# GpSimd sums pairs 0, 3, 4 and 5 of the attention probabilities, and the queries' second products of layer 0 come one pair of output tiles later

## The chip, the cores and the metric

The kernel runs on one core of a Trainium2 chip. A core has five engines that run their own instruction streams in order and wait for each other by semaphores: TensorE (PE in the profile, with its weight loads PEld), VectorE (DVE), ScalarE (ACT), GpSimd (POOL) and SyncE (SP), which here issues most of the transfers. The metric is the device time of one execution in microseconds. Before the change the median of three runs is 2087.75 us (2087.69 to 2091.03).

## The reference

One step of a two-layer trunk over 2048 latent tokens and 128 context tokens, width 1024, all in float32. Cut to what the change touches, layer 0 is:

```python
q_lat, kv_lat, k_pe, gate_a, pool_in, gate_b = jnp.split(h @ w_in, SPLITS_AB, axis=-1)
q = (rmsnorm(q_lat, q_norm) @ w_uq).reshape(B, T, MLA_HEADS, QK_NOPE + QK_ROPE)
ckv = rmsnorm(kv_lat, kv_norm)
...
s = (jnp.einsum('bqhd,bkhd->bhqk', qn, k_nope, preferred_element_type=jnp.float32)
     + jnp.einsum('bqhr,bkr->bhqk', qp, k_pe, preferred_element_type=jnp.float32))
p = jax.nn.softmax(s * sm_scale, axis=-1).astype(v.dtype)
return jnp.einsum('bhqk,bkhd->bqhd', p, v)
```

There are 4 heads, and each latent query sees 2048 latent and 128 context keys. `q_lat` has 256 columns and `w_uq` is the queries' second matrix. The softmax needs, for every query, the sum of its probabilities over 2176 keys. Layer 1 is a gated position-mixing block and is not touched.

## The kernel before

Activations are held with features on the 128 partitions and tokens along the row. Exact float32 products are made of three fast ones: every operand is split into a high part (a ScalarE cast) and a low part (a VectorE or GpSimd subtraction, `sub`, line 160), and `mm3` (lines 175 to 179) issues high x high, high x low and low x high.

Layer 0's projection goes over five blocks of tokens (512, 512, 512, 384, 256). In each, `linear` makes *output pairs*: two output tiles of 128 features in one double PSUM buffer (`psA`, two buffers of two banks), 48 products of 128x512 a pair. The order in a block is: keys' latent pair, queries' latent pair, then six more pairs (pooling input and two gates), which I number 1 to 6. After each of these six a hook runs: it lets every coroutine in `hold` (`kv_consume`, `q_consume`), the next block's preparation (`n`), the pooling (`p`) and the late modulation (`l`) take one step each. `q_consume` (line 529) normalises the queries' latent, splits it into `qh` (line 548) and `ql`, and then gives the queries' second products in three steps of 12 products, with a `yield` between the steps: heads 0 and 1, heads 2 and 3, and the rotary part. Each step takes a `psA` buffer, evacuates it by a ScalarE cast (line 561) and a VectorE subtraction, and SyncE stores the results to `q_d`. The pairs 1 to 6 are evacuated by ScalarE (line 591). Weights come in tiles of 512 KB through four raw buffers, split by line 423 (ScalarE) and line 160 (VectorE).

Attention then goes over 17 blocks: 16 of 512 latent queries of one head, and one for the context queries. A block has nine steps: eight *pairs* of key tiles (0 to 7, two tiles of 128 keys) and one single tile (the context keys of the cache). For a pair, TensorE makes the scores into `psA` (lines 820 to 824), ScalarE copies them to SBUF (line 835), and VectorE keeps a running maximum from PSUM (line 845), so a `psA` buffer is free only after both. When a block's scores are complete, TensorE turns the maximum (line 851), VectorE reduces it (853), TensorE spreads it over the partitions (859), VectorE subtracts it pair by pair (865) and ScalarE takes the exponent (867). All pairs but pair 4 are split for the product with the values: ScalarE casts (871), GpSimd subtracts (873). The products with the values run 14 steps behind the scores.

The sum of the probabilities is shared out: pairs in `POOL_SUM` (for the very first block `POOL_FIRST`) are added on GpSimd (lines 883 and 886) into one SBUF tile, the others on VectorE (889 and 892) into a PSUM bank (`psE`), and at the end VectorE adds GpSimd's part (896). The result is split, summed over the partitions by TensorE (921, 922), inverted on VectorE (295, 302, 303), and GpSimd multiplies it with the gate (928).

A scheduler of the framework sets the order on each engine from the program order and from when it thinks operands are there; each engine then runs its stream strictly in that order.

Of the kernel before, what the change touches and what calls it, by code (L numbers as in the profile page):

```python
# [12 lines left out]
ALU = mybir.AluOpType  # L13
# [68 lines left out]
AHEAD = 3  # L82
PT = 512
FIRST_W = (7, 9)
POOL_SUM = (1, 3, 4, 6)
POOL_FIRST = (1, 4)
SPLIT_PV = (0, 1, 2, 3, 5, 6, 7)
SPLIT_LAST = ()

# [24 lines left out]
def trunk_kernel(ctx, tc, xT, cols_in, cond_in, ident_in, edge_in, rope_in, w_ada, w_ada_T, w_in_t, w_inp_T, w_pool,  # L114
# [20 lines left out]
    def wt(dt=F32, shape=(P, 2, 512)):  # L135
        return wpool.tile(list(shape), dt, tag="w", name=nm("w"))
# [7 lines left out]
    def et(dt=F32, shape=(P, 2, 512)):  # L144
        return epool.tile(list(shape), dt, tag="e", name=nm("e"))
# [4 lines left out]
    def ps_pair(shape=(P, 2, 512)):  # L150
        return psA.tile(list(shape), F32, tag="A", name=nm("psA"))

    def ps1(tag, shape=(P, 512)):
        return psS.tile(list(shape), F32, tag=tag, name=nm("ps" + tag))

    def f(ap):
        return ap.bitcast(F32)

    def sub(eng, out, a, hi):
        eng.tensor_tensor(out=out, in0=a, in1=f(hi), op=ALU.subtract)  # L160

    V, S, G, PE = nc.vector, nc.scalar, nc.gpsimd, nc.tensor
# [3 lines left out]
    def store(c, *a):  # L166
        qs[c].dma_start(*a)

    def behind(ins, last):

        if last is not None:
            tc.add_manual_dep(ins.ins, last.ins.name, NO_SYNC, reason="issue order")
        return ins

    def mm3(ps, w, x, first, last):

        PE.matmul(ps, w[0], x[0], start=first, stop=False)  # L177
        PE.matmul(ps, w[0], x[1], start=False, stop=False)  # L178
        PE.matmul(ps, w[1], x[0], start=False, stop=last)  # L179
# [106 lines left out]
    def split1(x, n, alloc, lo_eng=None):  # L286

        t = alloc(F32R)
        S.copy(t[:, 0, :n], x)
        sub(lo_eng or V, t[:, 1, :n], x, t[:, 0, :n])  # L290
        return t
# [14 lines left out]
    def total(x, n, pool):  # L306

        if not pool:
            return split1(x, n, et)
        r = et()  # L310
        G.partition_all_reduce(r[:, 0, :n], x, P, bass_isa.ReduceOp.add)
        return r

    def rstd(r, n, d, pool, tag):

        if pool:
            return invert(r[:, 0, :n], r, n, 1.0 / d)
        ps = ps1(tag)
        PE.matmul(ps[:, :n], ones[1], r[:, 0, :n], start=True, stop=False)
        PE.matmul(ps[:, :n], ones[1], r[:, 1, :n], start=False, stop=True)  # L320
        return invert(ps[:, :n], et(), n, 1.0 / d)
# [166 lines left out]
    def rope(raw, n, ns, tab):  # L488

        t = et()  # L490
        if ns:
            V.stream_shuffle(t[:, 1, :ns], raw[:, :ns], [i ^ 16 for i in range(32)])
            V.tensor_tensor(out=t[:, 0, :ns], in0=raw[:, :ns], in1=tab[:, 0, :ns], op=ALU.mult)
            (G if ROPE_G else V).tensor_tensor(out=t[:, 1, :ns], in0=t[:, 1, :ns], in1=tab[:, 1, :ns], op=ALU.mult)
            V.tensor_tensor(out=t[:, 0, :ns], in0=t[:, 0, :ns], in1=t[:, 1, :ns], op=ALU.add)
        if ns < n:
            V.tensor_copy(out=t[:, 0, ns:n], in_=raw[:, ns:n])
        return t[:, 0, :n]
# [34 lines left out]
    def q_consume(bi, ps, tab):  # L533
        o, n = BLOCKS[bi]
        ns = min(n, DEC - o)
        q = et()
        S.copy(q[:, :, :n], ps[:, :, :n])
        sq = et()
        S.activation(out=sq[:, :, :n], in_=ps[:, :, :n], func=AF.Square)
        V.tensor_tensor(out=sq[:, 0, :n], in0=sq[:, 0, :n], in1=sq[:, 1, :n], op=ALU.add)  # L540
        hl = total(sq[:, 0, :n], n, AR_Q)
        yield
        r = rstd(hl, n, 256, AR_Q, "D")
        for a in range(2):
            V.scalar_tensor_tensor(out=q[:, a, :n], in0=q[:, a, :n], scalar=cols[:, C_QN + a:C_QN + a + 1],
                                   in1=r, op0=ALU.mult, op1=ALU.mult)
        qh = et(F32R)
        S.copy(qh[:, :, :n], q[:, :, :n])
        ql = et(F32R)
        sub(V, ql[:, :, :n], q[:, :, :n], qh[:, :, :n])  # L550
        yield
        for hp in range(2):
            if hp:
                yield
            pq = ps_pair()
            for a in range(2):
                for k in range(2):
                    mm3(pq[:, a, :n], (g.wc[0][:, k, 2 * hp + a], g.wc[1][:, k, 2 * hp + a]),
                        (qh[:, k, :n], ql[:, k, :n]), k == 0, k == 1)
            th = et(F32R)  # L560
            S.copy(th[:, :, :n], pq[:, :, :n])
            tl = et(F32R)
            sub(V, tl[:, :, :n], pq[:, :, :n], th[:, :, :n])
            for a in range(2):
                store(ST_QH, q_d[2 * hp + a, :, 0, o:o + n], f(th[:, a, :n]))
                store(ST_QL, q_d[2 * hp + a, :, 1, o:o + n], f(tl[:, a, :n]))
        yield
        pq = ps_pair()
        for hp in range(2):
            for k in range(2):  # L570
                mm3(pq[:, hp, :n], (g.wpe[0][:, k, hp], g.wpe[1][:, k, hp]),
                    (qh[:, k, :n], ql[:, k, :n]), k == 0, k == 1)
        raw = et()
        S.copy(raw[:, :, :n], pq[:, :, :n])
        for hp in range(2):
            pe = rope(raw[:, hp, :n], n, ns, tab)
            t = et(F32R)
            S.copy(t[:, 0, :n], pe)
            sub(V, t[:, 1, :n], pe, t[:, 0, :n])
            for a in range(2):  # L580
                for part in range(2):
                    store(ST_QP, q_d[2 * hp + a, 64 * part:64 * part + 64, 2, o:o + n], f(t[64 * a:64 * a + 64, part, :n]))
# [162 lines left out]
    for bi, (o, n) in enumerate(BLOCKS):  # L745
# [26 lines left out]
        linear(hh, n, 1, lambda p, ps: start(kv_consume, ps))  # L772
        hook(HOOK_KV)
        linear(hh, n, 1, lambda p, ps: start(q_consume, ps))
        drain(hold[0], 1)
        hook(HOOK_Q)
# [84 lines left out]
    def step_exp(b, p):  # L861

        nt = len(b.tiles[p])
        s = b.s[p]
        V.tensor_tensor(out=s[:, :nt], in0=s[:, :nt], in1=b.m[:, None, :].broadcast_to([P, nt, QB]),  # L865
                        op=ALU.subtract)
        S.activation(out=s[:, :nt], in_=s[:, :nt], func=AF.Exp, scale=SM_SCALE)  # L867
        b.parts[p] = low = None
        if p in (SPLIT_LAST if b.j == 15 else SPLIT_PV) and nt == 2:
            ph = wt(F32R)  # L870
            S.copy(ph[:, :nt], s[:, :nt])  # L871
            pl = wt(F32R)
            low = behind(G.tensor_tensor(out=pl[:, :nt], in0=s[:, :nt], in1=f(ph[:, :nt]), op=ALU.subtract), g.gated)  # L873
            b.parts[p] = ph, pl
        if p == 0:
            b.pool = b.acc = None
        last_p = len(b.tiles) - 1
        if nt == 1 and p == 0:
            b.total = s[:, 0]
        elif p in (POOL_SUM if b.j else POOL_FIRST):  # L880
            if b.pool is None:
                b.pool = et()
                behind(G.tensor_tensor(out=b.pool[:, 0], in0=s[:, 0], in1=s[:, 1], op=ALU.add), low)
            else:
                for a in range(2):
                    behind(G.tensor_tensor(out=b.pool[:, 0], in0=b.pool[:, 0], in1=s[:, a], op=ALU.add), low or g.gated)  # L886
        elif b.acc is None:
            b.acc = ps1("E")
            V.tensor_tensor(out=b.acc, in0=s[:, 0], in1=s[:, 1], op=ALU.add)
        else:  # L890
            for a in range(nt):
                V.tensor_tensor(out=b.acc, in0=b.acc, in1=s[:, a], op=ALU.add)
        if p == last_p:
            if b.acc is not None:
                b.total = b.acc
                V.tensor_tensor(out=b.total, in0=b.acc, in1=b.pool[:, 0], op=ALU.add)
            b.hl = split1(b.total, QB, et)
            b.gt = et()
            if b.h is not None:
                store(LD_GT, b.gt[:, 0], ga_d[b.h, :, b.t0:b.t0 + QB])  # L900
            else:
                dma(b.gt[:, 0].rearrange("p (h n) -> p h n", h=H), ga_d[:, :, DEC:T].rearrange("h p n -> p h n"))
# [39 lines left out]
    for j in range(16):  # L942
        b = Blk()
# [6 lines left out]
    b = Blk()  # L950
# [317 lines left out]
    for i in range(len(steps) + LAG + PV_BEHIND + 2):  # L1268
        if 0 <= i - LAG < len(steps):
            step_exp(*steps[i - LAG])  # L1270
# [5 lines left out]
        if i < len(steps):  # L1276
            b, p = steps[i]
# [13 lines left out]
        if 0 <= j < len(steps):  # L1291
            b, p = steps[j]
# [134 lines left out]
```

## Time and profile before

| what | value |
|---|---|
| runs | 2087.75 us median (2087.69 to 2091.03) |
| profiled execution: time, span | 2087.39 us, 2085.6 us |
| TensorE busy | 2001.2 us, 96% of the span |
| VectorE, ScalarE, GpSimd busy | 70%, 53%, 28% |
| mean granted TensorE clock | 0.989 |
| layer 0's projection, attention, the rest | about 0 to 515, 515 to 1095, 1095 to 2086 us |

The span runs from the first to the last instruction; 1.8 us of the execution lie around it. "Idle before" in a row is the time for which the engine had nothing to run just before, and the arrow names what ended it.

### The profile page before, as it was taken

What the parts mean: (1) busy time and instruction counts of PE and PEld (TensorE: products, weight loads), DVE (VectorE), ACT (ScalarE), POOL (GpSimd) and SP (SyncE); (2) the same over time, 40 slices, a digit from 0 to 9 for tenths busy, and PEclk for the clock granted to TensorE, in tenths of its full rate; (3) what the DMA queues carried; (4) which work ended last, traced back from release to release, by engine and by line L of the source; (5) the groups of instructions that cost most, each with busy time, mean ns of one, the idle gap of its engine ahead of it and who ended that gap; (6) DMA issues with size and microseconds to landing.
All of it is one profiled execution on the core that took longest, in us unless ns stands there. A gap on an engine that the chain in (4) does not pass through costs nothing.

```text
span 2085.6 us, 26154 instructions
## 1 busy us (share of the span) xinstructions
PE 2001.2 (96%) x9652; PEld 1666.0 (80%) x9652; DVE 1469.1 (70%) x2222; ACT 1098.6 (53%) x1285; POOL 580.7 (28%) x405
## 2 busy tenths in 40 slices
PE   6898999999999999999989999999999999999997
PEld 3787777998777777777758788888888888889997
DVE  4688977665887878878784898455665556477575
ACT  4634444544676767667664545443355335445555
POOL 1003020111478686868771120001101100010000
PEclk9999999999999999999999999999999999999999
DMA  9577767676111011101124564334524542364463
GB/s 355 191 259 244 242 226 233 211 227 191 45 31 47 30 46 31 46 30 33 49 86 162 174 210 147 116 131 162 172 83 141 190 142 101 122 224 160 129 222 126
DMA packets 123696, 300.62 MB, mean 144 GB/s; under 512 B 12144, under 2 KB 39088, under 8 KB 123568
## 3 DMA queue, kind: packets, MB, share of 16 engines
q1 hardware_dynamic: 105168, 258.58, 37.3%
q10 hardware_dynamic: 13728, 23.60, 3.7%
q0 software_dynamic: 4672, 16.78, 2.3%
q8 instruction: 76, 1.25, 0.2%
q14 instruction: 52, 0.43, 0.1%
HBM read 243.23 MB, written 55.67 MB: 143 GB/s over the span
## 4 chain that ended last, share of the span: by engine, by line
PE 66%; DVE 12%; POOL 7%; issue 5%; ACT 4%; DMA 3%; SPq 0%; DVEq 0%; POOLq 0%; ACTq 0%
PE psA L178 18%; PE psA L179 18%; PE psA L177 18%; POOL e L886 4%; DVE h L865 3%; POOL w L873 2%; DVE run L845 2%; DVE w L160 2%; PE psB L915 1%; ACT h L835 1%; PE psA L820 1%; PE psA L821 1%; PE psA L824 1%; PE psA L823 1%; PE psA L822 1%
## 5 line engine op out<-in xcount | busy, mean ns | idle before, releaser
L177 PE MATMUL psA<-h,w 128*128 128x512 f32 (+2 forms) x1600 | 575.7, 360 | 9.1 <-ACT e L591 6.6
L179 PE MATMUL psA<-h,w 128*128 128x512 f32 (+2 forms) x1600 | 573.2, 359 | 0.2 <-DVE w L160 0.2
L160 DVE TENSOR_TENSOR w<-r,w 128x1024 fp32r<-128x1024 f32 x280 | 349.2, 1250 | 291.4 <-PE psA L178 214.0
L178 PE MATMUL psA<-h,w 128*128 128x512 f32 (+2 forms) x1536 | 548.8, 357 | 2.0 <-DVE h L160 2.0
L423 ACT CAST w<-r 128x1024 fp32r<-128x1024 f32 x280 | 292.0, 1049 | 240.5 <-PE psA L179 189.2
L177 PEld LDWEIGHTS psA<-h,w 128*128 128x128 f32 x1600 | 302.9, 189 | 49.8 <-ACT e L591 7.3
L179 PEld LDWEIGHTS psA<-h,w 128*128 128x128 f32 x1600 | 302.8, 189 | 38.3 <-DVE w L160 0.4
L178 PEld LDWEIGHTS psA<-h,w 128*128 128x128 f32 x1536 | 290.9, 189 | 38.4 <-DVE h L160 3.1
L873 POOL TENSOR_TENSOR w<-h,w 128x1024 fp32r<-128x1024 f32 x105 | 252.1, 2402 | 132.4 <-ACT w L871 130.5
L845 DVE TENSOR_TENSOR run<-psA,run 128x512 f32<-128x512 f32 x240 | 163.4, 681 | 15.2 <-ACT h L835 14.5
L867 ACT ACTIVATE h<-h 128x1024 f32<-128x1024 f32 (+1 forms) x145 | 143.7, 1014 | 53.1 <-DVE h L865 52.9
L865 DVE TENSOR_TENSOR h<-h,psC 128x1024 f32<-128x1024 f32 (+1 forms) x145 | 163.5, 1145 | 0.9 <-PE psC L859 0.9
L835 ACT COPY h<-psA 128x1024 f32<-128x1024 f32 (+1 forms) x145 | 138.3, 964 | 34.1 <-PE psA L824 33.8
L178 PE MATMUL psA<-o,w 128*128 128x512 f32 (+2 forms) x368 | 134.0, 366 | 0.0
L886 POOL TENSOR_TENSOR e<-e,h 128x512 f32<-128x512 f32 x92 | 120.2, 1307 | 5.8 <-ACT h L867 2.2
L871 ACT CAST w<-h 128x1024 fp32r<-128x1024 f32 x105 | 110.5, 1054 | 11.0 <-PE psB L179 10.9
L639 POOL TENSOR_TENSOR pl<-pl 128x527 f32<-128x527 f32 (+2 forms) x16 | 22.0, 1374 | 329.4 <-PE psA L179 118.9
L179 PE MATMUL psA<-o,w 128*128 128x512 f32 (+2 forms) x304 | 109.1, 361 | 0.0
L177 PE MATMUL psA<-o,w 128*128 128x512 f32 (+2 forms) x304 | 108.9, 361 | 0.0
L177 PE MATMUL psA<-w,h 128*128 128x512 f32 x272 | 106.7, 393 | 1.2 <-ACT o L1147 1.2
L178 PE MATMUL psA<-w,h 128*128 128x512 f32 x272 | 106.1, 390 | 0.1
L179 PE MATMUL psA<-w,h 128*128 128x512 f32 x272 | 105.8, 390 | 0.0
(297 smaller groups left out, 3559.7 us busy)
## 6 DMA issues: line engine op xcount, KB each, us to landing
r<-in_w_inc_t_dram SPq DMA_DIRECT2D x80, 512.0 KB, 3.5
r<-in_w_in_t_dram SPq DMA_DIRECT2D x60, 512.0 KB, 4.1
r<-in_w_oap_t_dram SPq DMA_DIRECT2D x40, 512.0 KB, 3.4
r<-in_w_incv_t_dram SPq DMA_DIRECT2D x40, 512.0 KB, 4.1
r<-in_w_outc_t_dram SPq DMA_DIRECT2D x40, 512.0 KB, 3.5
r<-in_w_ada_T_dram SPq DMA_DIRECT2D x32, 512.0 KB, 4.5
r<-wp_d SPq DMA_DIRECT2D x20, 512.0 KB, 5.9
h<-in_w_ada_dram SPq DMA_DIRECT2D x16, 512.0 KB, 10.5
```

The lines of the kernel that those rows point to most:

```text
L160: eng.tensor_tensor(out=out, in0=a, in1=f(hi), op=ALU.subtract)
L177: PE.matmul(ps, w[0], x[0], start=first, stop=False)
L178: PE.matmul(ps, w[0], x[1], start=False, stop=False)
L179: PE.matmul(ps, w[1], x[0], start=False, stop=last)
L423: S.copy(hi, raw)
L835: S.copy(s[:, :nt], ps[:, :nt])
L845: V.tensor_tensor(out=b.max, in0=ps[:, a], in1=s[:, 0] if p == 0 else b.max, op=ALU.max)
L865: V.tensor_tensor(out=s[:, :nt], in0=s[:, :nt], in1=b.m[:, None, :].broadcast_to([P, nt, QB]), op=ALU.subtract)
L867: S.activation(out=s[:, :nt], in_=s[:, :nt], func=AF.Exp, scale=SM_SCALE)
L871: S.copy(ph[:, :nt], s[:, :nt])
L873: low = behind(G.tensor_tensor(out=pl[:, :nt], in0=s[:, :nt], in1=f(ph[:, :nt]), op=ALU.subtract), g.gated)
L886: behind(G.tensor_tensor(out=b.pool[:, 0], in0=b.pool[:, 0], in1=s[:, a], op=ALU.add), low or g.gated)
```

## The change

It has three parts. `POOL_SUM` becomes pairs 0, 3, 4, 5 (and `POOL_FIRST` 0 and 4), so GpSimd's tile begins with pair 0, VectorE's bank with pair 1, and GpSimd's last pair is 5 in place of 6. VectorE's first addition of a block, which added two SBUF tiles into `psE`, becomes a ScalarE copy of the first tile into `psE` and a VectorE addition of the second to it. And in `q_consume` one more `yield` stands ahead of the first step of the second products.

```diff
-POOL_SUM = (1, 3, 4, 6)
-POOL_FIRST = (1, 4)
+POOL_SUM = (0, 3, 4, 5)
+POOL_FIRST = (0, 4)
...
         ql = et(F32R)
         sub(V, ql[:, :, :n], q[:, :, :n], qh[:, :, :n])
+        yield
         yield
         for hp in range(2):
             if hp:
...
         elif b.acc is None:
             b.acc = ps1("E")
-            V.tensor_tensor(out=b.acc, in0=s[:, 0], in1=s[:, 1], op=ALU.add)
+            S.copy(b.acc, s[:, 0])
+            V.tensor_tensor(out=b.acc, in0=b.acc, in1=s[:, 1], op=ALU.add)
         else:
             for a in range(nt):
                 V.tensor_tensor(out=b.acc, in0=b.acc, in1=s[:, a], op=ALU.add)
```

Lines after the new `yield` are numbered one higher in the changed kernel, and those after the new copy two higher.

The first place is GpSimd in one attention block in the middle of the stage. `w` is the low part of a pair's probabilities (line 873, in the changed kernel 874), `h` a pair's probabilities, the `e` of lines 883 and 886 (884, 887) is GpSimd's sum, and the `e` of line 928 (930) the gate of the block before. Before:

```order
L873 TENSOR_TENSOR w_6077<-h_5721,w_6075 128x1024
L873 TENSOR_TENSOR w_6106<-h_5753,w_6104 128x1024
L883 TENSOR_TENSOR e_6108<-h_5753 128x512
L873 TENSOR_TENSOR w_6140<-h_5788,w_6138 128x1024
L928 TENSOR_TENSOR e_6045<-e_6045,e_6131 128x512
L873 TENSOR_TENSOR w_6177<-h_5817,w_6175 128x1024
L886 TENSOR_TENSOR e_6108<-e_6108,h_5817 128x512 x2
L886 TENSOR_TENSOR e_6108<-e_6108,h_5846 128x512
L873 TENSOR_TENSOR w_6233<-h_5884,w_6231 128x1024
L886 TENSOR_TENSOR e_6108<-e_6108,h_5846 128x512
L873 TENSOR_TENSOR w_6256<-h_5917,w_6254 128x1024
L886 TENSOR_TENSOR e_6108<-e_6108,h_5917 128x512 x2
```

And in the changed kernel, in the block at the same place:

```order
L874 TENSOR_TENSOR w_6082<-h_5725,w_6080 128x1024
L884 TENSOR_TENSOR e_6084<-h_5725 128x512
L874 TENSOR_TENSOR w_6111<-h_5757,w_6109 128x1024
L874 TENSOR_TENSOR w_6146<-h_5792,w_6144 128x1024
L930 TENSOR_TENSOR e_6050<-e_6050,e_6137 128x512
L874 TENSOR_TENSOR w_6183<-h_5821,w_6181 128x1024
L887 TENSOR_TENSOR e_6084<-e_6084,h_5821 128x512 x2
L887 TENSOR_TENSOR e_6084<-e_6084,h_5851 128x512 x2
L874 TENSOR_TENSOR w_6239<-h_5889,w_6237 128x1024
L887 TENSOR_TENSOR e_6084<-e_6084,h_5889 128x512 x2
L874 TENSOR_TENSOR w_6262<-h_5922,w_6260 128x1024
L874 TENSOR_TENSOR w_6294<-h_5949,w_6292 128x1024
```

GpSimd has the same 15 instructions a block; its sum is complete one line-874 subtraction earlier, ahead of the low part of pair 6.

The second place is ScalarE in a block after its maximum is known. `psA` of line 835 (836) are scores, line 867 (868) the exponents, 871 (872) the casts of pairs, `psE` VectorE's sum. Before:

```order
L867 ACTIVATE h_6546<-h_6546 128x1024
L835 COPY h_6888<-psA_6877 128x1024
L871 CAST w_6900<-h_6546 128x1024
L867 ACTIVATE h_6578<-h_6578 128x1024
L867 ACTIVATE h_6613<-h_6613 128x1024
L835 COPY h_6917<-psA_6906 128x1024
L871 CAST w_6929<-h_6578 128x1024
L867 ACTIVATE h_6642<-h_6642 128x1024
L871 CAST w_6963<-h_6613 128x1024
```

And in the changed kernel:

```order
L868 ACTIVATE h_6277<-h_6277 128x1024
L836 COPY h_6620<-psA_6609 128x1024
L872 CAST w_6632<-h_6277 128x1024
L868 ACTIVATE h_6309<-h_6309 128x1024
L868 ACTIVATE h_6344<-h_6344 128x1024
L836 COPY h_6649<-psA_6638 128x1024
L872 CAST w_6661<-h_6309 128x1024
L890 COPY psE_6665<-h_6309 128x512
L872 CAST w_6696<-h_6344 128x1024
```

The copy into `psE` stands behind the cast of pair 1, eighth from the exponent of pair 0; VectorE's addition that needs it stands in VectorE's stream behind the subtractions (line 866) of pairs 0 to 5.

The third place is TensorE in layer 0's second block. `psA_1561` is pair 2, the products on `wch` and `wcl` are the first step of the queries' second matrix, and the products on `h` and `w` of pair 3 follow. Before:

```order
L179 MATMUL psA_1561<-h_1017,w_1447 128x512
L521 MATMUL psD_1613<-ident,e_1277 128x128 x4
L177 MATMUL psA_1619<-e_1512,wch 128x512
L178 MATMUL psA_1619<-e_1514,wch 128x512
L179 MATMUL psA_1619<-e_1512,wcl 128x512
```

And in the changed kernel:

```order
L179 MATMUL psA_1561<-h_978,w_1447 128x512
L521 MATMUL psD_1613<-ident,e_1277 128x128 x4
L177 MATMUL psA_1664<-h_733,w_1551 128x512
L178 MATMUL psA_1664<-h_736,w_1551 128x512
L179 MATMUL psA_1664<-h_733,w_1553 128x512
```

Pair 3 (`psA_1664`) runs whole, 48 products, and the second products start behind it. On ScalarE its evacuation has moved too. Before, in the same block, from the cast of the first step's result on:

```order
L561 CAST e_1632<-psA_1619 128x1024
L361 ACTIVATE h_1642<-h_1284,mod 128x512 x2
L361 ACTIVATE h_1760<-h_1286,mod 128x512
L423 CAST w_1781<-r_1779 128x1024
L361 ACTIVATE h_1760<-h_1286,mod 128x512
L591 ACT_TABLE_LOAD
L591 ACTIVATE e_1734<-psA_1685 128x1024
```

And in the changed kernel, where line 592 evacuates pair 3:

```order
L423 CAST w_1660<-r_1658 128x1024
L361 ACTIVATE h_1621<-h_1284,mod 128x512 x2
L423 CAST w_1760<-r_1758 128x1024
L361 ACTIVATE h_1739<-h_1286,mod 128x512 x2
L592 ACT_TABLE_LOAD
L592 ACTIVATE e_1713<-psA_1664 128x1024
L562 CAST e_1729<-psA_1716 128x1024
```

The evacuation of pair 3 stands behind the same four activations of the next block's preparation (line 361) as before, while the cast of the first step's result has moved from ahead of them to behind it.

## Rows read from the trace of the kernel before

**Rows 1.** The page, its first line.

```profile
span 2085.6 us, 26154 instructions
```

**Rows 2.** Waits of TensorE, whole span: engine line waited for: us, times, longest.

```profile
PE psA L820 <- DVE run L845: 15.6, 30, 1.2
...
PE psA L177 <- ACT e L548: 7.8, 2, 5.9
...
PE psA L178 <- DVE e L160: 4.5, 3, 2.8
PE psB L178 <- POOL w L873: 3.2, 2, 2.6
```

**Rows 3.** Timeline, TensorE, attention: start, us, instruction, [idle before <- what ended it].

```profile
820.07 1.05 PE L859 MATMUL psC<-ident,s 128*128 128x128 f32 x8
821.53 0.50 PE L820 MATMUL psA<-r,K 128*128 128x512 f32 x1 [0.40 <-DVE run L845]
...
829.67 0.47 PE L820 MATMUL psA<-r,K 128*128 128x512 f32 x1 [0.59 <-DVE run L845]
...
837.88 0.39 PE L820 MATMUL psA<-r,Kb 128*128 128x512 f32 x1
```

**Rows 4.** Timeline, VectorE, the same block.

```profile
818.51 0.70 DVE L896 TENSOR_TENSOR psE<-psE,e 128x512 f32<-128x512 f32 x1 [5.26 <-POOL e L886]
...
823.03 2.34 DVE L865 TENSOR_TENSOR h<-h,psC 128x1024 f32<-128x1024 f32 x2
825.37 0.70 DVE L889 TENSOR_TENSOR psE<-h 128x512 f32<-128x512 f32 x1
...
828.84 0.68 DVE L845 TENSOR_TENSOR run<-psA,run 128x512 f32<-128x512 f32 x1
...
835.32 0.65 DVE L845 TENSOR_TENSOR run<-psA,run 128x512 f32<-128x512 f32 x1
```

**Rows 5.** Timeline, GpSimd, the same block.

```profile
805.83 4.09 POOL L886 TENSOR_TENSOR e<-e,h 128x512 f32<-128x512 f32 x3
809.88 2.41 POOL L873 TENSOR_TENSOR w<-h,w 128x1024 fp32r<-128x1024 f32 x1
...
815.82 2.65 POOL L886 TENSOR_TENSOR e<-e,h 128x512 f32<-128x512 f32 x2
...
837.91 1.30 POOL L928 TENSOR_TENSOR e<-e,e 128x512 f32<-128x512 f32 x1 [0.88 <-DVE e L303]
```

**Rows 6.** Timeline, ScalarE, the same block.

```profile
810.81 0.59 ACT L835 COPY h<-psA 128x512 f32<-128x512 f32 x1
...
829.88 1.05 ACT L871 CAST w<-h 128x1024 fp32r<-128x1024 f32 x1
```

**Rows 7.** Timeline, VectorE, layer 0.

```profile
185.37 1.53 DVE L540 TENSOR_TENSOR e<-e 128x512 f32<-128x512 f32 x1
...
209.48 1.23 DVE L160 TENSOR_TENSOR e<-e,e 128x1024 fp32r<-128x1024 f32 x1
```

**Rows 8.** Timeline, GpSimd, layer 0.

```profile
184.97 1.38 POOL L639 TENSOR_TENSOR pl<-pl 128x519 f32<-128x519 f32 x1 [6.51 <-DVE pl L655]
```

**Rows 9.** Timeline, TensorE, layer 0, blocks 0 and 1.

```profile
104.90 0.50 PE L177 MATMUL psA<-h,w 128*128 128x512 f32 x1 [3.71 <-ACT e L591]
...
209.50 0.80 PE L177 MATMUL psA<-e,wch 128*128 128x512 f32 x1 [5.91 <-ACT e L548]
...
229.04 0.40 PE L177 MATMUL psA<-h,w 128*128 128x512 f32 x1
```

**Rows 10.** Stretch, TensorE: length, busy (count), granted clock, DMA share, GB/s.

```profile
209.50:215.50 6.00, 5.54 (x13) 0.53 0.53 175
```

**Rows 11.** Stretch, VectorE, the same columns.

```profile
210.00:313.00 103.00, 87.79 (x151) 0.97 0.72 237
```

**Rows 12.** Timeline, ScalarE, layer 0, block 1.

```profile
226.55 1.28 ACT L591 ACT_TABLE_LOAD   x1 [3.05 <-PE psA L179]
227.85 1.03 ACT L591 ACTIVATE e<-psA 128x1024 f32<-128x1024 f32 x1
```

## The prediction

> **What bounds the kernel now.** I read the page's first line and busy shares, then TensorE's waits over the span, then a timeline of one attention block on four engines, then the waits of layer 0 on their timelines. The profiled execution took 2087.4 us, 0.4 below the median of the runs: its span of 2085.6 [rows 1] and 1.8 around it. The sum below is made against 2087.4. TensorE is busy for 96% of the span, so time can only come from its gaps, from stretches at a lower granted clock, or be lost by new gaps. Its largest group of gaps is line 820, scores waiting for the running maximum of line 845: 15.6 us in 30 waits [rows 2]. Two stand in a block, 0.40 at 821.53 and 0.59 at 829.67 [rows 3], and 30 are two in each of 15 blocks. In layer 0 the first products with the queries' second matrix wait 7.8 us for their high parts and 4.5 for their low parts [rows 2], the largest 5.91 at 209.50, and at 104.90 a pair waits 3.71 for an evacuation [rows 9]: together 16.0.
>
> Where do the waits on line 845 come from? VectorE stood for 5.26 us until 818.51 in front of line 896, which adds GpSimd's sum [rows 4]. GpSimd's last two additions begin at 815.82 and take 2.65 [rows 5], so they end at 818.47. From there VectorE has work without a gap up to the maximum at 828.84, whose end at 829.52 releases TensorE's scores of 829.67 [rows 3, 4]. VectorE waits early in the block, and TensorE pays late in it, because VectorE starts the block's burst with a backlog.
>
> **Pairs 0, 3, 4, 5.** GpSimd keeps its count of instructions. What changes is that no addition waits for pair 6: all are done ahead of that pair's low part, which takes 2.41 [rows 5]. So line 896 can follow about 2.4 us earlier, at 816.1 instead of 818.5 on the old clock. GpSimd also begins with pair 0's sum of 1.3 us (half of 2.65 [rows 5]) in time in which it idles now between the low parts of pairs 0 and 1. The burst behind line 896 then is no longer what TensorE waits for: 2.4 us of advance stand against waits of 0.40 and 0.59. What is late next? The subtractions of line 865 need line 859 of TensorE, which begins at 820.07 and takes 1.05 [rows 3]; they can begin at 821.1, and not at 823.03 [rows 4], because the maxima ahead of them were part of the backlog. That is 1.9 us, still more than 0.59. GpSimd's product with the gate, which waits 0.88 for VectorE's line 303 [rows 5], moves forward with it. I count all of 15.6, and give the term bounds of 12 and 17.6: below, if TensorE keeps a quarter of them; above, if small waits beside them go too.
>
> A second gap follows at the end of the stage: TensorE waits up to 2.6 us for GpSimd's last low part (3.2 in two waits [rows 2]). It comes earlier by the idle time that the first sum now fills, 1.3 us, and by the earlier line 303, up to 0.88 [rows 5]. I take 2.0, bounds 0 and 2.6.
>
> **The copy into psE.** VectorE's addition at 825.37, 0.70 long, stays as one addition; ScalarE gets one 128x512 copy more. No row shows such a copy into PSUM. The nearest is 0.59 for one out of PSUM [rows 6]; bounds 0 (hidden) and all that a late copy would hold. ScalarE is busy for about half of the time, so its own 0.59 costs nothing. What the copy can hold is VectorE: it stands behind the cast of pair 1, which begins at 829.88 and takes 1.05 [rows 6], so the copy would end at 831.5 on the old clock. With the subtractions 1.9 us earlier it ends near 829.6. VectorE reaches its addition behind six subtractions of 1.17 (2.34 for two) and four maxima of 0.6, near 821.1 + 7.0 + 2.4 = 830.5. So the copy is there, with 0.9 to spare. And if it isn't: behind the addition stand the maxima of pair 4, of which the last now ends at 835.97 (835.32 and 0.65 [rows 4]), 1.9 ahead of the scores of pair 6 at 837.88 [rows 3]. With 2.5 of advance, less about 1.0 (0.40 and 0.59) by which TensorE comes earlier, the slack there is 3.4. I take 0.
>
> A row bears on why the addition may want a PSUM operand. In layer 0 a VectorE addition of two SBUF tiles (line 540) took 1.53 us at 185.37 [rows 7], while GpSimd ran line 639 from 184.97 for 1.38 [rows 8]; it ended 0.55 after that one. Line 889, of the same kind and size, takes 0.70 at 825.37 [rows 4], where GpSimd is idle. The Trainium skill ("SBUF — State Buffer", section "SBUF: two separate sides") says that a VectorE instruction with two SBUF inputs and a GpSimd instruction that reads SBUF exclude each other for a whole instruction; the trace agrees. By that rule the old two-SBUF addition, moved to pair 1, would meet a low part of 2.4 us, inside the slack of 3.4: the sum would be the same with and without the copy.
>
> **The extra yield.** In the changed order pair 3 runs ahead of the second products, so their normalised input has a pair's time more. Pair 3 ran for about 11 us, from 215.5 to the end at 226.55 for which its evacuation waits [rows 10, 12]. That covers the 5.91 and the 0.46 behind it (209.50 is followed by another short wait, a part of the 4.5). While TensorE restarts, it also runs slow: from 209.5 to 215.5 the granted clock is 0.53, about the lower of its two levels, which costs 6.0 x (1 - 0.53) = 2.8 us [rows 10]. If all gaps go, and up to 2.8 behind each of the three large ones, that is 16.0 + 8.4 = 24.4: the ceiling.
>
> I don't take the ceiling, since another wait takes the place. Pair 4 needs the second psA buffer again, so pair 3's evacuation, and that stands on ScalarE behind four activations of line 361, which VectorE's line 357 feeds. VectorE ends `ql` at 209.48 + 1.23 = 210.7 [rows 7]. Behind it come 13 instructions up to the fourth line 357: two weight splits of about 1.15, ten of about 0.65, one of 0.15, together 8.9. Then one activation (0.7), the table load (1.28) and the evacuation (1.03) [rows 12]: 210.7 + 11.9 = 222.6. Before, pair 4 began at 229.04 [rows 9], and it had two steps of second products ahead of it, of which one (2.7, 12 of 48 products' 11 us) now runs behind pair 4: 226.3 to compare. That leaves 3.7, of which a new restart at the low clock takes 2.8: 0.9. What is added is how much earlier VectorE itself comes: it is busy for 87.8 of 103 us [rows 11], so of the 3.71 and the slow stretch behind it in block 0 (up to 2.8) it can follow with perhaps half, 3. In block 2 the same order stands with a smaller gap (2.8 is the longest on line 160 [rows 2]): 1. The last gap of 1.3 in block 3 goes. Sum 0.9 + 3 + 1 + 1.3, rounded to 6; bounds -3 (a longer wait for pair 3's evacuation, with its slow restart) and 24.4. I take the value near the lower end, since line 357's chain is a row of work that nothing shortens. The stores to `q_d` on SP come one pair later as well; attention begins long after them, so they cost nothing.
>
> **Sum.** 2087.4 - 15.6 - 2.0 - 6.0 + 0 = 2063.8, say 2064.
>
> **The rivals.**
> (a) Layer 0 gives its ceiling. For it: the gaps of 16.0 are plain, and VectorE has 15 us of idle time in a block. Against it: the walk above. 2087.4 - 17.6 - 24.4 = 2045.
> (b) Half the waits on line 845 stay, because VectorE's queue itself is full there (gapless for 11 us now), and layer 0 gives nothing. 2087.4 - 7.8 - 2.0 = 2078. For it: the changed order puts five subtractions nearly in a row. Against it: 1.9 us of advance against 0.59.
> (c) Slower: the copy into psE comes late. Its place is ScalarE's queue behind the cast of pair 1; should that cast have to wait for a low-part buffer that TensorE's products free, the copy slips by a step. A step is some 3.9 us (TensorE's 829.67 to 837.88 are two [rows 3], 4.1 each). VectorE at 830.5 would be held to about 829.6 + 2 x 4.1 = 837.8 by a slip of two, 7.3 late, which is 3.9 over the slack, of which I take a half in each of 16 blocks since later gaps of VectorE give some back: 31, with nothing gained on line 845: 2087.4 + 31 - 8 = 2110. It decides from 3.4 us of lateness on; by one slip (0.3 over the slack) the cost would be 5 and the time still below before.
> (d) It doesn't do what it says: line 896 waits as long, now for VectorE's own additions of pairs 6 and 7, which it gathers at the end of a block. The additions are as many as before (8 a block), so this would only move the wait; 2087.
>
> **Chances.** The forecast 0.58, with a range of its own from 2055 to 2077 (terms 12 to 17.6, 0 to 2.6, -3 to 12, of which not all fall to one side); (a) 0.15, (b) 0.15, (c) 0.06, (d) 0.06. The range 2049 to 2080 takes in the forecast, (b) and half of the way to (a). About 0.2%, 4.2 us, is what a measurement of this kernel can tell from no change. Faster by more: the forecast, (a) and (b), 0.88; within: (d), 0.06; slower: (c), 0.06.
>
> **What would show it.** In the changed profile: VectorE's idle time in front of line 898 shorter than 5.26 by 2 or more; TensorE's group of line 821 waiting for line 846 gone or under 3 us; GpSimd's last addition ended before pair 6's low part; no idle time on VectorE that ends with a ScalarE copy of line 890. In layer 0: no wait of line 177 on the high part `e`, and in block 1 a new one of the pair behind pair 3 on line 592. Wrong would be the forecast if line 891 waits for the copy in every block, if the waits on line 846 stay above 8 us, or if layer 0 ends later than now.

## The result and the profile after

The changed kernel takes 2057.52 us (median of five runs, 2053.45 to 2060.05) against 2088.28: a ratio of 0.9849, interval 0.9834 to 0.9863, or 31 us less. The forecast was 2064 (24 less), range 2049 to 2080. The profiled execution is the fastest of the five, 2053.45, so its trace shows 34 us less than the trace of before.

The page's first line, TensorE's waits over the span, and one line of its waits before that the rows don't show:

```profile
span 2051.7 us, 26144 instructions
```

```profile
PE psA L177 <- ACT e L592: 16.1, 4, 6.2
...
PE psA L821 <- DVE run L846: 5.8, 6, 1.8
...
PE psB L178 <- POOL w L874: 2.3, 2, 1.6
```

```profile
PE psA L177 <- ACT e L591: 6.6, 3, 3.7
```

Against [rows 2]: the group of line 845 (now 846) fell from 15.6 us in 30 waits to 5.8 in 6, the two groups of the queries' high and low parts (7.8 and 4.5) are gone, and the group on the evacuation of a pair grew from 6.6 us in 3 waits (line 591, the last line shown) to 16.1 in 4 (line 592).

I cut both spans at the same instructions of TensorE. First before, then after: attention from its first to its last spreading of a maximum (line 859, now 860), and the seam from there to the first line 320 of layer 1.

```profile
530.23:1065.24 535.01, 518.32 (x2239) 1.00 0.12 39
1065.24:1177.96 112.72, 107.21 (x421) 0.95 0.49 161
```

```profile
524.39:1036.86 512.47, 510.69 (x2239) 1.00 0.13 40
1036.86:1145.94 109.08, 104.27 (x421) 1.00 0.52 170
```

| stretch | before | after | difference |
|---|---|---|---|
| start, to line 319 in block 0 | 81.28 | 80.97 | -0.3 |
| from there to the same place in block 1 | 109.93 | 104.32 | -5.6 |
| block 1 to block 2 | 108.47 | 107.41 | -1.1 |
| block 2 to block 3 | 97.05 | 98.68 | +1.6 |
| block 3 to the first spreading of a maximum | 133.50 | 133.01 | -0.5 |
| attention | 535.01 | 512.47 | -22.5 |
| seam | 112.72 | 109.08 | -3.6 |
| the rest (the same order of instructions) | 907.64 | 905.76 | -1.9 |

The reader is to see two numbers in the attention rows. The same 2239 products took 518.32 us busy before and 510.69 after: of the 22.5 us, 14.9 were idle time that the profile showed and 7.6 stood in rows that it counts as busy. And the seam's granted clock rose from 0.95 to 1.00. The last row is no gain that can be told from scatter: TensorE's products there stand in one and the same order in all the kernels below, and the stretch took between 905.7 and 911.7 in their profiled runs.

One block of the changed kernel, answering to [rows 3 to 6]. TensorE (start, us, instruction; idle before would stand in brackets):

```profile
802.42 1.05 PE L860 MATMUL psC<-ident,s 128*128 128x128 f32 x8
803.23 0.48 PE L821 MATMUL psA<-r,K 128*128 128x512 f32 x1
...
810.60 0.39 PE L821 MATMUL psA<-r,K 128*128 128x512 f32 x1
```

VectorE and GpSimd:

```profile
797.47 0.70 DVE L898 TENSOR_TENSOR psE<-psE,e 128x512 f32<-128x512 f32 x1 [1.70 <-POOL e L887]
...
803.64 3.47 DVE L866 TENSOR_TENSOR h<-h,psC 128x1024 f32<-128x1024 f32 x3
...
808.76 0.68 DVE L846 TENSOR_TENSOR run<-psA,run 128x512 f32<-128x512 f32 x1
...
813.00 0.69 DVE L891 TENSOR_TENSOR psE<-psE,h 128x512 f32<-128x512 f32 x1
```

```profile
794.79 2.64 POOL L887 TENSOR_TENSOR e<-e,h 128x512 f32<-128x512 f32 x2
797.39 4.73 POOL L874 TENSOR_TENSOR w<-h,w 128x1024 fp32r<-128x1024 f32 x2
```

No bracket is left on TensorE. GpSimd's sum ends at 797.43 and its last two low parts follow it; VectorE waits 1.70 for it in place of 5.26. The maximum that released TensorE's scores 9.45 us behind line 859 (829.52 against 820.07) now ends 7.02 behind line 860 (809.44 against 802.42), and the scores that need it start at 8.18. Block for block the period is 34.15 in place of 35.68.

ScalarE's queue changed too. Before, then after:

```profile
819.24 0.59 ACT L289 CAST e<-psE 128x512 fp32r<-128x512 f32 x1 [6.72 <-DVE psE L896]
...
819.73 1.93 ACT L835 COPY h<-psA 128x1024 f32<-128x1024 f32 x2
```

```profile
796.79 1.01 ACT L836 COPY h<-psA 128x1024 f32<-128x1024 f32 x1 [1.76 <-PE psA L825]
798.20 0.59 ACT L289 CAST e<-psE 128x512 fp32r<-128x512 f32 x1 [0.40 <-DVE psE L898]
```

Before, the cast of the finished sum (line 289) stood ahead of two copies of scores, so GpSimd's late sum held VectorE, VectorE held ScalarE for 6.72, and ScalarE held the next block's scores. After, a copy of scores stands ahead of the cast. The diff doesn't say this; the framework's scheduler did it. On VectorE the copies show as two waits of 0.22 for line 835 ahead of the maxima at 820.78 and 821.69.

### The profile page after: what moved, and what is told of

It is laid out like the page before. It is cut to its first block, busy times and chain, and to the rows that moved or that the text cites. A ratio compares the mean times of both kernels' runs of the same rounds, so it can differ in the third digit from the quotient of the medians.

```text
span 2051.7 us, 26144 instructions
## 1 busy us (share of the span) xinstructions
PE 1986.3 (97%) x9652; PEld 1661.7 (81%) x9652; DVE 1467.2 (72%) x2222; ACT 1108.1 (54%) x1301; POOL 581.3 (28%) x405
## 4 chain that ended last, share of the span: by engine, by line
PE 78%; DVE 9%; DMA 4%; issue 3%; ACT 3%; POOL 1%; SPq 1%; DVEq 0%; ACTq 0%; POOLq 0%
PE psA L177 17%; PE psA L178 17%; PE psA L179 17%; PE psA L821 3%; PE psA L822 3%; PE psA L823 3%; PE psA L824 3%; PE psA L825 3%; PE psB L178 2%; PE psB L179 2%; PE psB L177 2%; PE psB L917 2%; DVE w L160 1%; DMA r<-wp_d 1%; PE psB L1173 1%
## 5 line engine op out<-in xcount | busy, mean ns | idle before, releaser
L177 PE MATMUL psA<-h,w 128*128 128x512 f32 (+2 forms) x1600 | 578.3, 362 | 17.8 <-ACT e L592 16.1
L177 PE MATMUL psA<-o,w 128*128 128x512 f32 (+2 forms) x304 | 108.9, 361 | 0.0
```

## The experiments

Theory A at the start: the parts add, and attention gains because GpSimd's last pair is 5 in place of 6.

**The sum without the yield.** The changed kernel with

```diff
         sub(V, ql[:, :, :n], q[:, :, :n], qh[:, :, :n])
-        yield
         yield
```

> The changed kernel without the extra yield: layer 0 runs in the order of before, attention in the order of after. Theory A (the parts add, and attention gains 22.5 us by itself between the first and the last turn of the maxima, 512.5 in place of 535.0): 2088.3 - 22.5 - 3.6 at the seam behind attention = 2062, with waits of 3.71 and 5.91 back in layer 0. Rival (attention gained because layer 0 ends earlier and leaves its queues emptier): attention over 520, 2070 or more.

Measured: 2063.99 us, ratio 0.9887 (0.987 to 0.9903); attention 512.5, seam 108.9. Attention has the order of the changed kernel and its length, whatever layer 0 does: the parts are apart, and the rival (attention over 520) is out.

**The yield alone.** The kernel before with

```diff
         sub(V, ql[:, :, :n], q[:, :, :n], qh[:, :, :n])
+        yield
         yield
```

> The kernel before with the extra yield alone: layer 0 in the order of after, attention in that of before. Theory A: layer 0 gains about 6 (its waits of 3.71 and 5.91 go, new ones of 6.2, 6.2 and 3.4 on the evacuation of pair 3 come), attention stays at 535: 2082. Rival (the layer 0 gain is given back when attention starts): 2087 to 2089.

Measured: 2086.87, ratio 0.9987 (0.9976 to 0.9998), attention 534.8. Its ten runs go from 2081.86 to 2089.93; the profiled one, 2082.94, has attention starting 7.7 us earlier than before. So the yield alone gives about 2 us by the median, while taken out of the changed kernel it costs 6 (2063.99 against 2057.52, in different sets of runs). Which of the two is its worth is open. In the traces attention starts 6 to 8 us earlier with the yield, whether the other parts are there or not (524.39 against 530.64 of the sum without the yield, 522.49 against 530.23). What the profiled run lost again stands behind the seam: 911.7 against 907.6 before, for the same products in the same order. By the scatter of that stretch from run to run, nothing shows that the yield did it; the rival gave the time rightly (2087), but its reason, that attention gives the gain back where it starts, isn't seen: attention is 534.8 against 535.0, the seam 112.1 against 112.7.

**No copy.** The changed kernel with

```diff
-            S.copy(b.acc, s[:, 0])
-            V.tensor_tensor(out=b.acc, in0=b.acc, in1=s[:, 1], op=ALU.add)
+            V.tensor_tensor(out=b.acc, in0=s[:, 0], in1=s[:, 1], op=ALU.add)
```

> The changed kernel with VectorE's first addition of two SBUF tiles back in place of the copy and the addition; pairs 0, 3, 4, 5 and the yield stay. The framework sets a slightly other order for it (GpSimd's sum of pair 4 is cut by a low part again). Theory A (the last pair, 5 in place of 6, makes the gain, and the copy is worth nothing): 2057 to 2062. Rival B (the addition meets GpSimd's low part of 2.4 us in each block, and the burst is late): the addition takes over 1.5 us, waits of 0.3 or more come back in TensorE, 2065 to 2080. Rival C (the copy carries the gain): 2078 or more.

Measured: 2058.9, ratio 0.9869 (0.9846 to 0.9892); blocks of 34.14. VectorE and GpSimd in a block:

```profile
810.55 1.50 DVE L890 TENSOR_TENSOR psE<-h 128x512 f32<-128x512 f32 x1
```

```profile
809.08 2.41 POOL L874 TENSOR_TENSOR w<-h,w 128x1024 fp32r<-128x1024 f32 x1 [4.10 <-ACT w L872]
```

The mechanism of rival B is there: the addition of two SBUF tiles takes 1.50 (mean of 16: 1.46) and not the 0.70 of [rows 4], and ends 0.56 after GpSimd's low part. In these blocks it costs nothing: the slack behind it covers 0.8 us. Attention as a whole is 513.6 against 512.5, and the difference lies in its first two blocks. Theory A's number held, and rival C (2078 or more) is out.

**The copy alone.** The kernel before, pairs 1, 3, 4, 6, with

```diff
-            V.tensor_tensor(out=b.acc, in0=s[:, 0], in1=s[:, 1], op=ALU.add)
+            S.copy(b.acc, s[:, 0])
+            V.tensor_tensor(out=b.acc, in0=b.acc, in1=s[:, 1], op=ALU.add)
```

> The kernel before with the copy alone: pairs 1, 3, 4, 6 and no extra yield. The order on GpSimd differs from before by one place: pair 4 is added ahead of the low part of pair 5 in one piece. Theory A (GpSimd's last pair decides): VectorE still waits 4 to 5.3 us for GpSimd's sum of pair 6, TensorE's two waits a block stay, 2085 to 2090. Rival C (the copy, and the order that comes with it, carries the gain): 2062 to 2070.

Measured: 2072.00, ratio 0.9922 (0.9907 to 0.9937). Theory A (2085 to 2090) was wrong here: 17 us come without moving a pair, 14 of them in attention (521.0). Rival C had the direction and fell 2 us short of its range (2062 to 2070). VectorE:

```profile
811.38 0.70 DVE L897 TENSOR_TENSOR psE<-psE,e 128x512 f32<-128x512 f32 x1 [5.68 <-POOL e L886]
...
812.58 0.68 DVE L845 TENSOR_TENSOR run<-psA,h 128x512 f32<-128x512 f32 x1
...
820.22 0.68 DVE L845 TENSOR_TENSOR run<-psA,run 128x512 f32<-128x512 f32 x1
```

TensorE in the same block:

```profile
812.72 1.16 PE L859 MATMUL psC<-ident,s 128*128 128x128 f32 x8
...
820.77 0.39 PE L179 MATMUL psB<-w,Vl 128*128 128x512 f32 x1
821.05 0.47 PE L820 MATMUL psA<-r,K 128*128 128x512 f32 x1
```

VectorE still waits 5.68 for GpSimd, longer than before, and yet TensorE shows no wait on line 845 in these blocks. What went with the copy are three things in the order: the cast of line 289 no longer stands ahead of both score copies; the first maximum stands ahead of the sum's low part; and the first addition (0.70) stands behind the two maxima of pair 2 and not ahead of them. No run moves one of the three alone. The maximum that TensorE needs ends 8.18 behind line 859, not 9.45. Blocks take 34.6: the last 0.45 over 34.15 stand in no bracket. The largest part, 0.1 to 0.2, lies ahead of line 859, which here starts 0.44 behind the product before it (at 812.28) where the spacing is 0.23; 0.1 lies in line 859 itself, 1.16 in place of 1.05, and the rest around the scores at 821.05, which start 0.28 behind the product before them.

So a second theory, D: with the copy in place, the last pair is worth the 0.45 a block that are left.

**Last pair 6, and first pair 1.** Two kernels, each the changed kernel with one of

```diff
-POOL_SUM = (0, 3, 4, 5)
+POOL_SUM = (0, 3, 4, 6)
...
-POOL_SUM = (0, 3, 4, 5)
-POOL_FIRST = (0, 4)
+POOL_SUM = (1, 3, 4, 5)
+POOL_FIRST = (1, 4)
```

> The changed kernel with pairs 0, 3, 4, 6: the first pair as in the change, the last as before; copy and yield stay. Theory D (GpSimd's last pair sets when line 898 can run, and with the copy in place its lateness costs a block of attention 34.6 in place of 34.15, as in the kernel with the copy alone): VectorE waits 5 to 5.7 us for GpSimd in a block, blocks of 34.5 to 34.7, attention 520, 2064 to 2067. Rival E (that GpSimd begins with pair 0 makes the gain): wait under 3 us, blocks of 34.15, 2056 to 2060.

> The changed kernel with pairs 1, 3, 4, 5 (and 1, 4 for the very first block): the last pair as in the change, the first as before; copy and yield stay. Theory D: blocks of 34.15, attention 512 to 514, 2056 to 2060. Rival E: VectorE's wait for GpSimd back at 4 us or more, blocks of 34.4 or more, 2062 or more.

Measured: 2060.30, ratio 0.9876 (0.9849 to 0.9903), and 2059.21, ratio 0.9866 (0.9844 to 0.9888). Both have blocks of 34.14, and attention of 514.6 and 514.1. Theory D fell, and so did rival E: with the copy, either end of the list moved by one pair is enough. VectorE with last pair 6:

```profile
801.88 0.70 DVE L898 TENSOR_TENSOR psE<-psE,e 128x512 f32<-128x512 f32 x1 [3.76 <-POOL e L887]
```

Put on one clock, the start of line 859 (860) in the same block, six kernels make one picture:

| kernel | the sum's last addition (896, 898) ends | mean block |
|---|---|---|
| copy alone: 1, 3, 4, 6 | 0.64 before it | 34.6 |
| before: 1, 3, 4, 6, no copy | 0.86 before it | 35.7 |
| 0, 3, 4, 6 | 1.92 before it | 34.14 |
| 0, 3, 4, 5, no copy | 2.58 before it | 34.14 |
| 1, 3, 4, 5 | 3.60 before it | 34.14 |
| the change: 0, 3, 4, 5 | 4.25 before it | 34.15 |

There is a loop once around per block: subtractions, exponents, GpSimd's sums, VectorE's last addition, and what stands behind that addition in VectorE's queue. In the four rows from 1.92 on the loop has time to spare: TensorE's own 34.15 sets the period, and how much is spare doesn't matter, since VectorE's wait for GpSimd may be 1.70 or 3.76. In the first two rows the loop is longer than that, and it reaches TensorE by two different ways. The profile's chain of work, followed back through 770 to 860 from each step to what released it, shows them (start, us, what). Before:

```profile
818.51 0.71 DVE psE L896
819.73 1.94 ACT h L835 x2
821.69 0.70 DVE run L845
...
829.67 0.47 PE psA L820
...
841.80 1.06 ACT w L871
842.91 1.31 POOL e L886
...
854.17 0.71 DVE psE L896
```

The copy alone:

```profile
811.38 0.70 DVE psE L897
812.08 0.60 DVE s L853
812.72 1.16 PE psC L859 x8
```

Before, the last addition holds ScalarE's cast of line 289 and the two copies behind it, these hold VectorE's maxima, the maxima hold TensorE's scores at 829.67, and from there the chain comes back to GpSimd's sum and to the next last addition, 35.66 later. Line 859 isn't held: it starts 0.23 behind the product before it, as a product does that doesn't wait, and 0.27 behind the end of the reduction (line 853). With the copy alone the cast is out of that way, and the addition holds the reduction behind it, and this line 859, which starts 0.06 behind the reduction's end. So the first two rows can't be put in order by their first column. The last addition has come forward by 3.4 in the change; a kernel with the copy that has 1.1 of it (the 1.92) already runs at 34.14, and no run tells how little would do.

**Five raw buffers.** The changed kernel with

```diff
-NR = 4
-NH = 17
+NR = 5
+NH = 16
```

This run and those after it ask what the new wait of layer 0 hangs on. TensorE, and ScalarE in block 1, in the changed kernel:

```profile
218.78 0.80 PE L177 MATMUL psA<-h,w 128*128 128x512 f32 x1 [6.23 <-ACT e L592]
...
324.39 0.79 PE L177 MATMUL psA<-h,w 128*128 128x512 f32 x1 [6.17 <-ACT e L592]
...
414.27 0.68 PE L177 MATMUL psA<-h,w 128*128 128x384 f32 x1 [3.41 <-ACT e L592]
```

```profile
208.83 1.39 ACT L361 ACTIVATE h<-h,mod 128x512 fp32r<-128x512 f32 x2 [4.23 <-DVE h L357]
214.11 1.04 ACT L423 CAST w<-r 128x1024 fp32r<-128x1024 f32 x1 [3.89 <-DMA r<-in_w_in_t_dram]
215.06 1.33 ACT L361 ACTIVATE h<-h,mod 128x512 fp32r<-128x512 f32 x2
216.41 1.28 ACT L592 ACT_TABLE_LOAD   x1
217.70 1.02 ACT L592 ACTIVATE e<-psA 128x1024 f32<-128x1024 f32 x1
```

> The changed kernel with five raw weight buffers in place of four, paid for with 16 in place of 17 buffers for scores; the order of TensorE and GpSimd is nearly the same. Theory F (the new waits of 6.2, 6.2 and 3.4 in layer 0 last as they do because a weight tile arrives late, its transfer being issued only when VectorE's second weight split frees a buffer; ScalarE's cast of it stands ahead of the evacuation of pair 3): ScalarE's wait of 3.9 for the transfer in block 1 goes, the waits of TensorE shrink to 2 to 4 each, 2050 to 2054. Rival G (VectorE's line 357 holds the evacuation, as the prediction has it): waits as long as before, 2056 to 2059. Risk: with 16 score buffers ScalarE's copies in attention wait for one, and attention is longer than 512.5.

Measured: 2050.92, ratio 0.983 (0.9806 to 0.9854). TensorE's waits, and ScalarE in block 1:

```profile
213.94 0.80 PE L177 MATMUL psA<-h,w 128*128 128x512 f32 x1 [6.56 <-ACT e L592]
...
319.42 0.50 PE L177 MATMUL psA<-h,w 128*128 128x512 f32 x1 [2.11 <-ACT e L592]
...
406.85 0.45 PE L177 MATMUL psA<-h,w 128*128 128x384 f32 x1 [1.33 <-ACT e L592]
```

```profile
206.38 0.73 ACT L361 ACTIVATE h<-h,mod 128x512 fp32r<-128x512 f32 x1 [5.17 <-DVE h L357]
207.01 1.03 ACT L423 CAST w<-r 128x1024 fp32r<-128x1024 f32 x1
```

The cast no longer waits for its tile, and in blocks 2 and 3 the waits shrink to 2.11 and 1.33: theory F. In block 1 the wait stays, on line 357: rival G. Both hold, in different blocks. The same kernel, run again below, has 6.61, 2.02 and 1.38. The risk named, a longer attention for want of a score buffer, isn't shown: 513.8 here, 512.5 in the second run.

**Preparation later.** The changed kernel with, in the hook (its order is `'hnpl'` else),

```diff
+                if bi and turns[0] == 3:
+                    order = 'hpl'
+                if bi and turns[0] == 4:
+                    order = 'hnnpl'
```

> The changed kernel, in which the next block's preparation skips its step behind pair 3 and takes two behind pair 4 (blocks 1 to 4): pair 3's evacuation stands behind two activations of line 361 in place of four. Theory F: the cast that waits for its weight tile still stands ahead, so only the two activations of 0.66 go, 1.3 in each of blocks 1 to 3: 2053 to 2056. Rival G (line 357's chain holds it): the waits shrink by 3 us each, 2048 to 2051. Risk: the preparation comes late for the next block, with a wait at its start, 2058 or more.

Measured: 2059.87, ratio 0.9863 (0.9835 to 0.989): no gain over the changed kernel. In block 1 the cast still waits, 4.70, for its tile, and TensorE 5.54; block 2's wait fell to 3.21. But the stretch from block 1 to block 2 is 112.3 us in place of 107.4, with a new wait of 4.5 on line 295, which belongs to the norm at a block's start. The risk named came true.

**Late modulation later.** The kernel with five raw buffers and, in the hook,

```diff
+                if bi in (1, 2) and turns[0] in (2, 3):
+                    order = 'hnp'
+                if bi in (1, 2) and turns[0] in (4, 5):
+                    order = 'hnpll'
```

Beside it on the same chip the changed kernel and the one with five raw buffers, unchanged.

> The kernel with five raw buffers, and in blocks 1 and 2 the late modulation (line 266 on VectorE) skips its step behind pairs 2 and 3 and takes two behind pairs 4 and 5. Three additions of line 266 leave VectorE's stretch between the low part of the queries' latent and line 357. Theory G (with the weight tile there in time, line 357's chain alone holds pair 3's evacuation in block 1): TensorE's wait of 6.56 falls to 3.5 to 4.5, 2046 to 2050. Rival (the late modulation then is not done by block 3 and stands there in one piece, or VectorE is as late by other work): 2051 or more.

> The changed kernel again, on the same chip as the two others of this call: 2054 to 2060.

> The kernel with five raw buffers again, beside the changed kernel: if its gain is real, 5 to 8 us below that one; if it was the chip's, within 2.

Measured: 2052.21 (ratio 0.9821, 0.9806 to 0.9837), 2058.18 (0.9856, 0.9838 to 0.9875) and 2055.39 (0.9832, 0.9814 to 0.985). My expectation (2046 to 2050, a wait of 3.5 to 4.5 in block 1) was wrong, and the rival's time came: TensorE's wait there grew to 10.23. VectorE in that stretch:

```profile
205.44 0.68 DVE L654 SCALAR_TENSOR_TENSOR pl<-pl,pl 128x504 f32<-128x504 f32 x1 [2.40 <-POOL pl L649]
```

With line 266 out of the way the pooling is next in VectorE's queue, and waits for GpSimd ahead of line 357. Block 2 has hardly a wait left (0.19). The five raw buffers gain 2.8 us over the changed kernel in this set, between the 5 to 8 and the 2 that I had set as the marks of a real gain and of none; by the medians of two sets it was 6.6. With the late modulation moved as well it is 6.0, and the interval just doesn't touch that of the changed kernel (0.9837 against 0.9838), but it overlaps that of the five raw buffers alone. In the traces attention starts at 516.9 and 521.9 with the five raw buffers, at 519.2 with the late modulation moved too, and at 524.4 and 525.5 in the changed kernel. So a gain of 0.1 to 0.3% from the five raw buffers is likely, and the late modulation's own worth isn't shown.

## Why the prediction was right, point by point

The size of the whole was right (24 forecast, 31 measured), and the mechanism of attention was right in its direction and incomplete in its cause.

**Attention: 15.6 forecast, 22.5 measured.** Two errors against each other. I said that the 30 waits are two in each of 15 blocks. They aren't: 25 lie between 615 and 1044 (12.5 us), and 5 at the start of the stage, which stayed (6 waits of 5.8 after), so that my sign for this group, gone or under 3 us, wasn't met. And I priced a wait at the idle time that its row shows. A block lost 0.99 by the brackets and 1.53 by its period. The rest is in the rows: the products follow each other every 0.227, but a row lasts 0.39, so a gap shows only what it has beyond 0.16, and the product behind a gap takes 0.31 to 0.33 to the next. That is the 7.6 us of busy time that went, about 0.3 for each wait. The upper bound of 17.6 was too low for this reason.

**GpSimd's sum** came earlier as said; VectorE's wait fell from 5.26 to 1.70, and in the chain of work before, the sum does stand ahead of TensorE's scores. That this wait by itself was the cause is what the copy alone refutes: with 5.68 of it the two waits of TensorE are gone. The step that was wrong is the way from the sum to TensorE. I wrote that VectorE has work without a gap from line 896 to the maximum at 828.84; it stands twice, 0.22 each, for ScalarE's copies, which stood behind the cast of line 289. That cast and two places in VectorE's own order are the three more parts of the backlog, and the prediction looked at none of them: the pieces of ScalarE's order that I had printed begin behind that cast, and I read them for the copy's own lateness only.

**The copy at 0**: right for its cost (0.596 on ScalarE, no wait on line 890), wrong for its worth. With it comes another order, which is worth 14 us of attention (535.0 to 521.0) where the pairs stay, and about 1 where they move (513.6 to 512.5).

**The rule of the Trainium skill on two SBUF operands** ("SBUF — State Buffer", "SBUF: two separate sides"): the run without the copy agrees, 1.46 against 0.70; that the sum is the same with and without held too, 2058.9 against 2057.5.

**The seam: 2.0 forecast, 3.6 measured, by another way.** One wait of 2.64 for GpSimd's low part became two, 0.67 and 1.64, so hardly any of the 2.0 came. TensorE's idle time in the seam fell by 0.7 (from 5.5 to 4.8); the other 2.9 lie in the busy time of the same 421 products, with a granted clock of 1.00 in place of 0.95. I counted the wait and not the clock. The kernel without the copy, with 0.97, kept a seam of 111.9.

**Layer 0: 6 forecast; 5.8 by the start of attention (530.23 to 524.39).** The sum was right by luck, since the errors of its terms cancel. Block 0 kept all of 5.6 (I took 3); block 1 gave 1.1 (0.9); block 2 lost 1.6 (I took a gain of 1); from block 3 on it was 0.5 (1.3). The wait that I put in the place of the old one is there, on the line and at the pair named. I had pair 4 at 11.9 behind the end of `ql`; it starts at 218.78, and `ql` ended at 202.7: 16.1. The 4.2 missing have two parts. VectorE with the changed kernel, then with five raw buffers:

```profile
211.85 1.40 DVE L357 SCALAR_TENSOR_TENSOR h<-h,amul,e 128x512 f32<-128x512 f32 x2
```

```profile
209.40 1.40 DVE L357 SCALAR_TENSOR_TENSOR h<-h,amul,e 128x512 f32<-128x512 f32 x2
```

The fourth line 357 ends 10.6 behind `ql` where I had 8.9: 1.7 of it. From there to pair 4 it takes 5.5 where I had 3.0: the other 2.5 are the cast that waits 3.89 for a weight tile and one more activation behind it. The cast stands in the changed order printed ahead of the prediction, but I hadn't it in the chain. The five raw buffers confirm the second part (3.1 from the fourth line 357 to pair 4), but there `ql` ends at 199.3 and VectorE's chain takes 11.5, so pair 4 comes 14.7 behind it and the wait stays. The new restarts run at a low clock as the old did:

```profile
218.70:225.00 6.30, 6.22 (x18) 0.65 0.94 328
```

**The rivals.** (a) didn't come, since three new waits stand in the place of the old. (c) and (d) didn't: line 891 starts at 813.00 without a wait, and the copy isn't late. In (c) a slip of one step is 829.6 + 4.1 = 833.7, 3.2 behind 830.5 and so 0.2 inside the slack of 3.4, not 0.3 over it. (b) is what the copy alone would have been near to in time, by another way: nothing of the waits' brackets stayed there, only 0.45 a block.

## What to carry to other kernels

A wait of an engine for a slow helper is a cost only where the loop through both is longer than the bounding engine's own period; write down when each link ends against one landmark of that engine, for several variants, and look for the threshold, since past it every further gain is free and worthless. Short of it, follow the chain of work back, since the same late helper can reach that engine by more than one way. Where a scheduler sets the order, an edit that looks like a change of cost is first a change of order on every engine: run each part alone before a part is credited. And a short gap of TensorE cost more here than its bracket: compare the busy time of the same instructions, or the period, not the sum of the idle times.

## What was not expected of the hardware

A TensorE gap shown as 0.40 or 0.59 cost 0.65 or 0.75 us against the spacing of products, and about 0.1 more behind it. A loss of 0.45 us a block can be made of no shown gap at all (the copy alone). And runs of one kernel, with one order of instructions, spread by 2 to 14 us here. In the profiled ones this lies outside attention, whose length repeats within 0.1 us (512.47, 512.54, 512.52, 512.52 in four of the runs with the changed attention; with five raw buffers it was 513.81 and then 512.51).
